# T4's weight parts split behind the first tile's B22, attention differences on VectorE, w_out's scaling at other ticks, and attention's closing additions behind a reciprocal

## The chip, the cores and the metric

One Trainium2 chip, one of its cores. The time is the device time of one execution in microseconds (us). A core has TensorE (PE, the matmuls; its weight loads are listed as PEld), VectorE (DVE), ScalarE (ACT), GpSimd (POOL), a queue engine SyncE (SP) and 16 DMA engines.

## The reference

One layer of a decoder trunk on x of 2048 rows and 1024 columns, all in fp32 (16 query heads, 2 key and value heads of width 64, window 128):

```python
shift, scale, gate = jnp.split(jax.nn.silu(c) @ w_ada + b_ada, 3, axis=-1)
u = x * (1.0 + scale) + shift
q, k, v, a_gate, p_in, p_gate, m_a, m_p = jnp.split(u @ w_in, offsets, axis=-1)
a = (sliding_window_sink_attention(q, k, v, sinks, bias, mask) * silu(a_gate)) @ w_attn_proj
p = einsum("bsgc,gcd->bsgd", multiscale_causal_pool(p_in), w_pool_mix)
p = ((p * pool_scale) * silu(p_gate)) @ w_pool_proj
y = ((sigmoid(m_a) * a + sigmoid(m_p) * p) @ w_out) * (1.0 + gate)
out = layer_norm(alpha * x + y, ln_gain, ln_bias)
```

## The kernel before

**Products.** Every large matrix product is computed in quads: two weight tiles of 128 columns against two halves of 512 rows of activations, with seven block products instead of eight: B11, T1, T2, B21, T3, B22, T4. Each is `product`: twelve fp32r matmuls of 128x512, because weights and activations are both split in a high and a low part (high by high, high by low, low by high). Twelve matmuls at full clock take 2.72 us. The weights come as a tile `W` (four blocks, three of which are made from differences by `sum1`, `mid` and `late` on POOL) and a tile `A22` (for T4). `pair_split` splits the weights of two products at once: ACT casts the high part into a `w_set` buffer (L303), and DVE makes the low part (L132, 128x1024). `half_split` does the same for one T4 (L310 and L132, 128x512). Products accumulate in banks of PSUM that the programs call `mm` and `lg` by their tags (four and two banks). Within a quad, T2 ends with the addition b = c + p5 (L365) and T3 with p5 = c + p5 (L387), both on DVE; T3 and T4 go on in the bank c.

**The order.** In `front` PE runs B11 and T1 of the two quads of a group, in `back` T2 and B21 of both, then T3 and B22 of the first, T3 and B22 of the second, and T4 of both. `ring` runs `front` of the next group behind `back`. The work of the other engines stands in program order on each engine; `tick` runs the side work (hooks) between products, `defer` moves a call some ticks on. A call of nc.vector, nc.scalar or nc.gpsimd may be moved by the tile scheduler; the wrapped ones (L57) keep their order.

**Stages, by the trace.** A head to 62 us, the first phase (gates of half 0) to 252, attention of half 0 to 600, the second phase to 830, attention of half 1 to 1178, then six phases: the last gates, the attention projection of half 0 (to 1290), the pool projection of half 0 (to 1370), the same two of half 1 (to 1448 and 1529), and the output product with LayerNorm. The four projection phases have two groups of two quads each. In them `take` on DVE multiplies the results by gates into tiles `wide`, the pool phases with two operations (L624 into `g`, L626 into `wide`), and DVE also makes the low parts of the next phase's activations (`set_B`, `set_T`).

**Attention.** 64 steps of two heads by 128 queries per half, with parts of steps n, n-1, n-2 and n-3 in flight at once. In a step, DVE runs: the reciprocal of the sums (`sm`), two additions into `o`, two maximum reductions over scores (`CUSTOM_DVE_ANT_0`), the low part `ptl` of the transposed probabilities, and the scaling of one head's probabilities (`L<-L,sm`). Beside the attention, `filling` runs products of other quads, a quarter product (three matmuls) at a time, five or six to a step; their weights are split by `split` (ACT, and POOL or DVE). Their two closing additions stand in `ended`, that is, in the program directly behind the last quarter of T2 or T3. `later(n, f)` runs f at the end of step n. `sums_between` is one such: at three places in each attention it fetches a row pair of the attention result into two `room` tiles and forms four differences of 128x512 (`sums_to`, on POOL: T1, T2, T4, T3), which are stored for the next phase.

**w_out.** In the second phase `sums_to` also prepares w_out in four parts (wo0 to wo3): two row blocks each are fetched into `spare`, multiplied by the gate row `cb` on DVE (`spare<-spare,cb`, 128x1024, twice per part), stored, and subtracted on POOL. The ticks at which the parts start are the last four numbers of a list.

## Time and profile before

| | |
|---|---|
| median of 3 runs | 1691.07 us (1689.7 to 1692.35) |
| the profiled execution, and its span | 1694.21 us, 1692.1 us |
| PE busy | 1645.3 us (97% of the span), 8058 matmuls |
| DVE busy | 1190.4 us (70%) |
| ACT busy | 1024.3 us (61%) |
| POOL busy | 968.4 us (57%) |
| mean granted PE clock | 0.997 of full speed |
| HBM | 197 GB/s over the span |

Busy time counts instructions that run, and with matmuls that are pipelined their ends are modelled. In the timeline a row gives the start, the time, the engine, the line, the operation, its output and inputs, and in square brackets the idle time ahead of it and the instruction that ended it. A row such as `lg<-set_T,w_set ... x12` is one block product. Line numbers from 205 on stand up to 14 higher in the kernel after the change (L132 and L57 stay, L615 becomes L620, L586 becomes L591).

### The profile page before, as it was taken

Reading aid. Unit: us, or ns where it says so; the run is one execution under the profiler, and the core shown is the slowest. Engines: PE = TensorE matmul, PEld = TensorE weight load, DVE = VectorE, ACT = ScalarE, POOL = GpSimd, SP = SyncE. Lnnn points to the kernel's source line nnn. Section 1 sums busy time; section 2 is a strip of 40 time slices with the busy share of each in tenths; the row PEclk is TensorE's granted clock in tenths of the full one; section 3 lists DMA queues with packets and bytes.
Section 4 is the critical chain, followed back from the end, with each engine's and each line's share of the span. In section 5 each row is a group of like instructions: output and inputs, shape, how many; then the busy total and the mean of one; then the engine's idle time right before and its main releaser. Section 6 shows DMA issues by size and latency. Waiting matters only on the chain.

```text
span 1692.1 us, 24664 instructions
## 1 busy us (share of the span) xinstructions
PE 1645.3 (97%) x8058; PEld 1383.4 (82%) x8058; DVE 1190.4 (70%) x2132; ACT 1024.3 (61%) x2146; POOL 968.4 (57%) x734
## 2 busy tenths in 40 slices
PE   7999999999999999999999999999999999999997
PEld 6788888888888788878888888887877878787886
DVE  6845656677767666486567677675768896978777
ACT  4754547877777655335578777776746454544452
POOL 3333437685867948764476768598444463323442
PEclk9999999999999999999999999999999999999999
DMA  9688844333442688872533345345957885676443
GB/s 360 218 281 301 206 152 139 97 123 115 159 148 69 223 280 295 290 260 101 167 112 107 111 127 179 106 148 186 357 201 272 290 307 193 238 276 232 150 150 112
DMA packets 185969, 331.55 MB, mean 196 GB/s; under 512 B 18016, under 2 KB 43760, under 8 KB 185840
## 3 DMA queue, kind: packets, MB, share of 16 engines
q1 hardware_dynamic: 182720, 325.72, 56.3%
q10 hardware_dynamic: 3088, 4.23, 1.2%
q8 instruction: 64, 1.05, 0.2%
q14 instruction: 65, 0.53, 0.1%
q0 software_dynamic: 32, 0.02, 0.0%
HBM read 223.77 MB, written 109.28 MB: 197 GB/s over the span
## 4 chain that ended last, share of the span: by engine, by line
PE 76%; DVE 9%; ACT 5%; DMA 4%; issue 3%; POOL 2%; SPq 1%; POOLq 0%; DVEq 0%; ACTq 0%
PE mm L57 49%; PE lg L57 20%; PE pv L57 4%; PE pt L57 3%; DVE set_T L57 1%; DMA ma_d<-raw 1%; DVE w_set L132 1%; ACT L L57 1%; DMA g<-ma_d 1%; DVE w_set L57 1%; ACT w_set L57 1%; DVE g L624 1%; SPq L57 1%; DVE L L57 1%; DVE qs L57 1%
## 5 line engine op out<-in xcount | busy, mean ns | idle before, releaser
L57 PE MATMUL mm<-set_B,w_set 128*128 128x512 f32 x2664 | 653.2, 392 | 0.6 <-DVE w_set L57 0.5
L57 PEld LDWEIGHTS mm<-set_B,w_set 128*128 128x128 f32 x2664 | 496.6, 188 | 103.0 <-DVE w_set L57 0.9
L57 PE MATMUL mm<-set_T,w_set 128*128 128x512 f32 x1824 | 453.9, 395 | 8.1 <-DVE mm L57 6.0
L57 PE MATMUL lg<-set_T,w_set 128*128 128x512 f32 x1704 | 413.8, 392 | 14.3 <-DVE w_set L132 12.4
L57 PEld LDWEIGHTS mm<-set_T,w_set 128*128 128x128 f32 x1824 | 335.9, 188 | 77.8 <-DVE mm L57 11.5
L57 PEld LDWEIGHTS lg<-set_T,w_set 128*128 128x128 f32 x1704 | 319.9, 189 | 86.5 <-DVE w_set L132 16.3
L132 DVE TENSOR_TENSOR w_set<-W,w_set 128x1024 fp32r<-128x1024 f32 x137 | 193.5, 1413 | 141.8 <-ACT w_set L303 131.8
L303 ACT CAST w_set<-W 128x1024 fp32r<-128x1024 f32 x137 | 143.8, 1050 | 195.1 <-PE mm L57 146.0
L266 POOL TENSOR_TENSOR W<-W,A 128x512 f32<-128x512 f32 x46 | 74.3, 1615 | 273.9 <-DMA A<-in_win_dram 65.2
L57 POOL TENSOR_TENSOR w_set<-W,w_set 128x512 fp32r<-128x512 f32 x120 | 157.5, 1320 | 100.3 <-ACT w_set L57 93.7
L57 DVE TENSOR_TENSOR o<-pv,o 64x128 f32<-64x128 f32 x256 | 72.0, 281 | 134.9 <-ACT o L57 128.4
L57 POOL TENSOR_TENSOR W<-W 128x512 f32<-128x512 f32 x82 | 108.3, 1335 | 46.3 <-DVE sm L57 25.6
L57 ACT ACTIVATE L<-L,nm 128x257 f32<-128x257 f32 (+1 forms) x256 | 127.2, 499 | 12.4 <-DVE nm L57 3.6
L275 POOL TENSOR_TENSOR W<-W 128x512 f32<-128x512 f32 x46 | 72.1, 1566 | 103.3 <-DVE w_set L132 91.5
L57 DVE CUSTOM_DVE_ANT_0 L<-lg,bt,nsink 128x256 f32<-128x256 f32 (+1 forms) x256 | 111.6, 473 | 20.2 <-PE lg L57 7.1
L270 POOL TENSOR_TENSOR W<-W 128x512 f32<-128x512 f32 x44 | 75.3, 1714 | 78.1 <-DVE w_set L132 69.0
L57 ACT CAST w_set<-W 128x512 fp32r<-128x512 f32 (+1 forms) x165 | 101.8, 628 | 27.7 <-POOL W L57 16.7
L57 ACT COPY o<-pv 64x256 f32<-64x256 f32 x128 | 47.3, 369 | 78.6 <-PE pv L57 77.5
L271 POOL TENSOR_TENSOR W<-W 128x512 f32<-128x512 f32 x44 | 69.2, 1572 | 33.2 <-DMA W<-in_win_dram 20.3
L57 DVE TENSOR_TENSOR ptl<-pt,pth 128x512 fp32r<-128x512 f32 (+1 forms) x128 | 85.6, 669 | 1.3 <-ACT pth L57 1.0
L57 POOL TENSOR_TENSOR spare<-spare 128x512 f32<-128x512 f32 x48 | 77.6, 1623 | 11.6 <-ACT spare L57 5.7
L57 ACT ACTIVATE L<-L,sm 128x256 f32<-128x256 f32 (+1 forms) x128 | 64.3, 502 | 31.5 <-DVE sm L57 31.2
(233 smaller groups left out, 2419.0 us busy)
## 6 DMA issues: line engine op xcount, KB each, us to landing
W<-in_win_dram SPq DMA_DIRECT2D x42, 512.0 KB, 5.9
W<-in_win_dram SPq DMA_DIRECT2D x42, 256.0 KB, 4.1
A<-in_win_dram SPq DMA_DIRECT2D x42, 256.0 KB, 4.8
ag_d<-sig SPq DMA_DIRECT2D x32, 256.0 KB, 5.3
pg_d<-sig SPq DMA_DIRECT2D x32, 256.0 KB, 5.0
pg<-pg_d SPq DMA_DIRECT2D x32, 256.0 KB, 3.3
pin_B<-fin SPq DMA_DIRECT2D x32, 256.0 KB, 2.1
ag<-ag_d SPq DMA_DIRECT2D x32, 256.0 KB, 2.9
```

Source lines behind the costliest of these rows:

```text
L57: return lambda *args, **kw: self.tc.keep_in_program_order(op(*args, **kw))
L132: engine.tensor_tensor(dst, src, as32(hi), ALU.subtract)
L266: e.tensor_tensor(self.w[:, 1, :], self.w[:, 2, :], self.a22, ALU.add)
L270: e.tensor_tensor(x[:, 1, :], x[:, 1, :], x[:, 0, :], ALU.subtract)
L271: e.tensor_tensor(x[:, 2, :], x[:, 0, :], x[:, 2, :], ALU.subtract)
L275: e.tensor_tensor(x[:, 3, :], x[:, 3, :], x[:, 1, :], ALU.subtract)
L303: a.copy(by_two(hi), raw)
L624: nc.vector.tensor_tensor(g, src, g, ALU.mult)
```

## The change

It has four parts.

1. `back`: where a group's quads have `ahead` (the two projections, both halves: phases 1 to 4 of the last six), both T4s' weights are split between the first quad's B22 and the second quad's T3, and the second quad's `third` pair ahead of the first's B22. Elsewhere the order stays. PE's order is the same everywhere.
2. In the attentions the four differences of `sums_between` run on DVE, their ticks are rounded up instead of down, and the second of the three places starts a step earlier.
3. The closing additions in attention are put in a list `closing` by `filling`; `close` issues them directly behind the reciprocal of the next step, or ahead of the next T3 or T4 if they are still in the list by then.
4. The four parts of w_out start at 33, 36, 43 and 48 instead of 34, 39, 44 and 50, and the second scaling of a part comes 1.5 ticks behind the first instead of 0.5. The same offset holds for the one other user of `work`, the modulation of x in the first phase.

```diff
--- before.py
+++ after.py
@@ -196,7 +196,7 @@
     def put(q, store, name, i, src):
         q.dma_start(store[name][i // 2, :, i % 2, :], src)
 
-    def sums_to(ph, store, i, load, work=None):
+    def sums_to(ph, store, i, load, work=None, eng=pool):
 
         b = []
 
@@ -210,11 +210,11 @@
                 load(b[r], r)
 
         def sub(out, a, c):
-            return lambda: pool.tensor_tensor(x(*out), x(*a), x(*c), ALU.subtract)
+            return lambda: eng.tensor_tensor(x(*out), x(*a), x(*c), ALU.subtract)
 
         todo = [(0, fetch)]
         if work:
-            todo += [(4, lambda: work(b[0], 0)), (4.5, lambda: work(b[1], 1))]
+            todo += [(4, lambda: work(b[0], 0)), (5.5, lambda: work(b[1], 1))]
         made = [("B11", (0, 0)), ("B21", (1, 0)), ("B22", (1, 1))] if work else []
         puts = [(5 + 0.6 * n, *x) for n, x in enumerate(made)]
         at = 7.5 if work else 4
@@ -393,15 +393,20 @@
             tick()
             q.consume(ph, 0, 1, b)
 
-        for x in range(len(st)):
-            third(x)
-            with_t3(x)
-            with_b22(x)
-        for q in nxt[len(st) :]:
-            ask(q)
+        lasts = []
+        third(0)
+        with_t3(0)
+        if grp[0].ahead:
+            third(1)
+            with_b22(0)
+            lasts = [half_split(ph, q.a22) for q in grp]
+        else:
+            with_b22(0)
+            third(1)
+        with_t3(1)
+        with_b22(1)
         for q, b, c, p5 in st:
-            w = half_split(ph, q.a22)
-            product(c, w, "T4")
+            product(c, lasts.pop(0) if lasts else half_split(ph, q.a22), "T4")
             tick()
             q.consume(ph, 1, 0, c)
 
@@ -929,25 +934,33 @@
             if name == "T1":
                 p5 = st[x][3] = tp.tile([P, CH], F32, tag="p5", bufs=2, name="p5")
                 act.copy(p5, b)
-            elif name == "T2":
-                dve.tensor_tensor(b, c, p5, ALU.add)
-            elif name == "T3":
-                dve.tensor_tensor(p5, c, p5, ALU.add)
             elif name == "B21":
                 take(x, 0, 0, a)
             elif name == "B22":
                 take(x, 0, 1, b)
-            else:
+            elif name == "T4":
                 take(x, 1, 0, c)
                 take(x, 1, 1, p5, True)
+
+        closing = []
+
+        def close():
+            while closing:
+                x, name = closing.pop()
+                _, b, c, p5 = st[x]
+                dve.tensor_tensor(b if name == "T2" else p5, c, p5, ALU.add)
 
         def filling():
             for i, (x, name) in enumerate(seq):
                 begun(i)
+                if name in ("T3", "T4"):
+                    close()
                 w = made.pop(i)
                 acc = st[x][{"B11": 0, "B21": 0, "T1": 1, "B22": 1}.get(name, 2)]
                 for k in range(4):
                     product(acc, w, name, name in ("B11", "T1"), k, k + 1)
+                    if k == 3 and x < K and name in ("T2", "T3"):
+                        closing.append((x, name))
                     yield
                 ended(i)
 
@@ -994,13 +1007,13 @@
             split(j)
 
         def sums_between(n0, i):
-            for offset, f in [(0, rooms), *sums_to(ph, ain_d[s], i, load_raw(ain_d[s], i))]:
-                later(n0 + int(offset / 2), f)
+            for offset, f in [(0, rooms), *sums_to(ph, ain_d[s], i, load_raw(ain_d[s], i), eng=dve)]:
+                later(n0 + math.ceil(offset / 2), f)
 
         def rooms():
             ph.turns["spare"] = iter([kvp.tile([P, D], F32, tag=f"qs0{t}", name=f"room{t}") for t in range(2)])
 
-        for i, n0 in enumerate((39, 56, 61)):
+        for i, n0 in enumerate((39, 55, 61)):
             sums_between(n0, i)
         fill = filling()
         lgs, exps, Ls, pvs, outs, ags = {}, {}, {}, {}, {}, {}
@@ -1018,6 +1031,7 @@
             if n - 1 in exps:
                 sm = exps[n - 1][2]
                 dve.reciprocal(sm, sm)
+            close()
             if n - 3 in pvs:
                 pv = pvs.pop(n - 3)
                 jj, tt, bb = (n - 3) // U, (n - 3) // NB % 2, (n - 3) % NB
@@ -1497,7 +1511,7 @@
                 lambda x, r: dve.tensor_tensor(x, x, cb, ALU.mult),
             ))
         ahead, hooks = hooks, {}
-        for start, todo in zip((14, 18, 22, 26, 30, 34, 39, 44, 50), side):
+        for start, todo in zip((14, 18, 22, 26, 30, 33, 36, 43, 48), side):
             for offset, f in todo:
                 at = int(start + offset) - 14
                 hooks.setdefault((at // 14, at % 14), []).append(f)
```

On DVE in the last group of the attention projection of half 0 (around 1280 us), the split of the two T4 weights (`w_set<-A22`) stood behind T3's additions of the first and the second quad (p5_13167 and p5_13215; W_13030 is the second quad's third pair):

```order
L387 TENSOR_TENSOR p5_13167<-lg_13168,p5_13167 128x512
L132 TENSOR_TENSOR w_set_13306<-W_13030,w_set_13305 128x1024
L615 TENSOR_TENSOR wide5_12572<-p5_13167,g_13161 128x512
L57 TENSOR_TENSOR set_T1_67<-set_T1_67 128x2x512
L615 TENSOR_TENSOR wide4_12571<-mm_13092,g_13206 128x512
L57 TENSOR_TENSOR set_T2_234<-set_T2_234 128x2x512
L387 TENSOR_TENSOR p5_13215<-lg_13216,p5_13215 128x512
L132 TENSOR_TENSOR w_set_13347<-A22_12990,w_set_13347 128x512
L615 TENSOR_TENSOR wide7_12574<-p5_13215,g_13165 128x512
L57 TENSOR_TENSOR set_T2_234<-set_T2_234 128x2x512
L615 TENSOR_TENSOR wide6_12573<-mm_13130,g_13210 128x512
L132 TENSOR_TENSOR w_set_13367<-A22_13031,w_set_13367 128x512
```

and now, with W_13015 in the place of W_13030 and A22_13016 of A22_13031:

```order
L132 TENSOR_TENSOR w_set_13289<-W_13015,w_set_13288 128x1024
L57 TENSOR_TENSOR set_B11_66<-set_B11_66 128x2x512
L387 TENSOR_TENSOR p5_13167<-lg_13168,p5_13167 128x512
L57 TENSOR_TENSOR set_T1_67<-set_T1_67 128x2x512
L620 TENSOR_TENSOR wide5_12572<-p5_13167,g_13161 128x512
L132 TENSOR_TENSOR w_set_13314<-A22_12990,w_set_13314 128x512
L620 TENSOR_TENSOR wide4_12571<-mm_13092,g_13206 128x512
L132 TENSOR_TENSOR w_set_13317<-A22_13016,w_set_13317 128x512
L57 TENSOR_TENSOR set_T2_234<-set_T2_234 128x2x512
L387 TENSOR_TENSOR p5_13215<-lg_13216,p5_13215 128x512
```

The third pair of the second quad stands ahead of the first T3's addition instead of behind it, and both low parts for T4 stand ahead of the second T3's addition; the gate products of the second quad (wide7, wide6) come behind.

On DVE at the 36th reciprocal of the first attention (439.83 us), the closing addition of a T2 (`mm_4471<-mm_4473,p5_4526`; sm_4515 are the sums of that reciprocal) stood at the end of the step, behind the scaling of L:

```order
L57 TENSOR_TENSOR ptl_4570<-pt_4556,pth_4569 128x512
L57 TENSOR_SCALAR L_4513<-L_4513,sm_4515 128x256
L57 TENSOR_TENSOR mm_4471<-mm_4473,p5_4526 128x512
L57 SCALAR_TENSOR_TENSOR fin_4468<-fin_4468,mm_4129 128x512
L57 RECIPROCAL sm_4574<-sm_4574 128x2
```

and now it stands behind the step's reciprocal, ahead of the additions into o:

```order
L57 TENSOR_SCALAR L_4439<-L_4439,sm_4441 128x256
L57 SCALAR_TENSOR_TENSOR fin_4384<-fin_4384,vb_4376 128x512
L57 RECIPROCAL sm_4515<-sm_4515 128x2
L57 TENSOR_TENSOR mm_4471<-mm_4473,p5_4526 128x512
L57 TENSOR_TENSOR o_4504<-pv_4543,o2_4565 64x128 x2
L57 ISA L_4573,nm_4574<-lg_4551,bt_3952,nsink_71 128x256
```

It has moved ahead by one step's work on DVE, which follows it in the same order.

On DVE in the second phase around 746 to 760 us, in the group of k, v and the first q, the two scalings of wo3 (`spare<-spare,cb`) stood behind the low part of W_7567 (the second quad's first pair, `front`):

```order
L132 TENSOR_TENSOR w_set_7646<-W_7519,w_set_7645 128x1024
L586 TENSOR_SCALAR sig_7593<-sig_7593,psc_72 128x512
L586 TENSOR_SCALAR sig_7621<-sig_7621,psc_72 128x512
L132 TENSOR_TENSOR w_set_7683<-W_7567,w_set_7682 128x1024
L586 TENSOR_SCALAR sig_7642<-sig_7642,psc_72 128x512
L57 TENSOR_TENSOR spare_7614<-spare_7614,cb_6526 128x1024
L57 TENSOR_TENSOR spare_7613<-spare_7613,cb_6526 128x1024
L132 TENSOR_TENSOR w_set_7726<-W_7519,w_set_7725 128x1024
L132 TENSOR_TENSOR w_set_7776<-W_7567,w_set_7775 128x1024
```

and now, with W_7523 and W_7579 in the place of W_7519 and W_7567:

```order
L132 TENSOR_TENSOR w_set_7648<-W_7523,w_set_7647 128x1024
L591 TENSOR_SCALAR sig_7603<-sig_7603,psc_72 128x512
L57 TENSOR_TENSOR spare_7572<-spare_7572,cb_6526 128x1024
L57 TENSOR_TENSOR spare_7571<-spare_7571,cb_6526 128x1024
L591 TENSOR_SCALAR sig_7625<-sig_7625,psc_72 128x512
L132 TENSOR_TENSOR w_set_7689<-W_7579,w_set_7688 128x1024
L591 TENSOR_SCALAR sig_7644<-sig_7644,psc_72 128x512
L132 TENSOR_TENSOR w_set_7729<-W_7523,w_set_7728 128x1024
L132 TENSOR_TENSOR w_set_7778<-W_7579,w_set_7777 128x1024
```

They stand two gate rows and one low part earlier, ahead of the second quad's first pair instead of behind it, and still next to each other.

## Prediction

> **What bounds the kernel.** I read the page's busy shares first, then PE's waits, then the windows around the places where the waits lie, then the timeline at each.
>
> ```profile
> PE 1645.3 (97%) x8058; PEld 1383.4 (82%) x8058; DVE 1190.4 (70%) x2132; ACT 1024.3 (61%) x2146; POOL 968.4 (57%) x734
> ```
>
> PE is the bound, and no matmul is added or removed. So the change can only give or take PE's idle time and slow clock. PE's waits (what PE waited for: us in total, times, longest):
>
> ```profile
> PE lg L57 <- DVE w_set L132: 12.4, 9, 2.8
> PE pv L57 <- DMA head_qs<-in_wadat_dram: 7.9, 1, 7.9
> PE mm L57 <- DVE mm L57: 6.0, 5, 2.1
> PE pt L57 <- DMA head_B<-in_wadat_dram: 3.1, 1, 3.1
> PE mm L57 <- DVE sm L57: 2.1, 1, 2.1
> PE pv L57 <- DVE ptl L57: 1.5, 4, 0.6
> ```
>
> The two DMA waits are the head, which isn't touched. The first line (a low part that DVE makes) is what parts 1 and 4 aim at; the third and fifth (T3 waits for T2's closing addition) are part 3's. Here the first line's large members stand: PE at the T4s of the attention projection of half 0 (1280), the pool projection (1363), the same of half 1 (1442, 1521).
>
> ```profile
> 1277.66 2.88 PE L57 MATMUL mm<-set_B,w_set 128*128 128x512 f32 x12
> 1280.38 1.98 PE L57 MATMUL lg<-set_T,w_set 128*128 128x512 f32 x8
> 1284.47 5.51 PE L57 MATMUL lg<-set_T,w_set 128*128 128x512 f32 x16 [2.11 <-DVE w_set L132]
> ...
> 1363.81 3.06 PE L57 MATMUL lg<-set_T,w_set 128*128 128x512 f32 x12 [1.30 <-DVE w_set L132]
> 1368.55 1.20 PE L57 MATMUL lg<-set_T,w_set 128*128 128x512 f32 x4 [1.68 <-DVE w_set L132]
> ...
> 1442.54 3.03 PE L57 MATMUL lg<-set_T,w_set 128*128 128x512 f32 x12 [0.26 <-DVE w_set L132]
> 1446.57 1.21 PE L57 MATMUL lg<-set_T,w_set 128*128 128x512 f32 x4 [1.00 <-DVE w_set L132]
> ...
> 1521.35 3.06 PE L57 MATMUL lg<-set_T,w_set 128*128 128x512 f32 x12 [1.01 <-DVE w_set L132]
> 1527.18 2.08 PE L57 MATMUL lg<-set_T,w_set 128*128 128x512 f32 x4 [2.77 <-DVE w_set L132]
> 1529.05 3.56 PE L57 MATMUL mm<-set_B,w_set 128*128 128x512 f32 x12
> ```
>
> Each T4 stops after its eight high matmuls, because the low part isn't there. Twelve matmuls last 2.88 us, yet the next product starts 2.72 behind (1280.38 less 1277.66), so a row's end lies 0.16 past the point where PE could go on: each stall costs its bracket and 0.16 more. Two stalls have a tail. After 1284.47, sixteen matmuls take 5.51 where the pitch of 0.227 (2.72 over 12) gives 3.79, and after 1527.18 the 2.08 and 3.56 stand against 1.07 (2.88 less eight times 0.227) and 2.88: 1.7 us more each. The windows (us, then busy time and instructions of PE, PEld, DVE, ACT and POOL, the granted clock, DMA share, GB/s) show why:
>
> ```profile
> 1275.00:1301.00 26.00, 23.89 (x99) 19.31 (x98) 23.35 (x20) 11.49 (x14) 13.06 (x8) 0.93 0.94 335
> 1345.00:1381.00 36.00, 33.02 (x145) 26.65 (x144) 35.13 (x36) 20.50 (x28) 15.91 (x9) 1.00 0.94 339
> 1433.00:1460.00 27.00, 25.75 (x112) 20.62 (x112) 25.02 (x23) 15.97 (x22) 11.81 (x7) 1.00 0.79 284
> 1512.00:1543.00 31.00, 27.22 (x112) 21.77 (x111) 28.84 (x28) 14.18 (x18) 11.45 (x8) 0.94 0.93 333
> 1284.40:1288.00 3.60, 3.53 (x9) 2.78 (x10) 3.60 (x6) 2.59 (x3) 0.00 (x0) 0.54 1.05 398
> 1527.10:1531.00 3.90, 3.82 (x10) 3.09 (x11) 3.47 (x5) 0.00 (x0) 1.27 (x1) 0.57 0.98 339
> ```
>
> In the two short windows the granted clock was 0.54 and 0.57. In the four long ones DVE is full or nearly so: 2.65, 0.87, 1.98 and 2.16 us are free. So at these places DVE's queue, not PE, sets the pace, and an earlier low part pushes something else back.
>
> **Part 1, T4's low parts earlier.** The four places lose 2.11 + 0.16 + 1.7 = 3.97, then 1.30 + 1.68 + 0.32 = 3.30, then 0.26 + 1.00 + 0.32 = 1.58, and 1.01 + 2.77 + 0.32 + 1.7 = 5.80: 14.65 in all, the ceiling of this part. Nothing is added; both low parts now stand ahead of the second T3's closing addition, which T4 of the second quad needs, and of the gate products and the next front's low part, which stood between or behind them. In the attention projections (1280 and 1442) DVE has 2 to 2.65 us free and the gate products there take one operation per result, so I take nearly all: 3.7 and 1.5. In the pool projections a result takes two operations, the same work stays in the stretch, and the wait partly changes its name: the second T4 waits for the second T3's addition, then the front for its low part. With 0.87 free at 1345 I take half, 1.7; at 1512, with 2.16 free and the clock's 1.7 regained if no single stall is as long as 2.1, I take 3.5. Together 10.4 (4 if DVE's queue gives back only its free time and no clock, 14.65 if all goes). ACT's casts for the T4s move up too, ahead of two casts for `set_T2`; at 44% to 59% busy ACT has the room.
>
> **Part 3, closing additions.** The first attention's example, DVE and then PE:
>
> ```profile
> 439.83 0.16 DVE L57 RECIPROCAL sm<-sm 128x2 f32<-128x2 f32 x1
> 440.83 0.58 DVE L57 TENSOR_TENSOR o<-pv,o 64x128 f32<-64x128 f32 x2 [0.84 <-ACT o L57]
> ...
> 442.87 1.39 DVE L57 TENSOR_SCALAR L<-L,sm 128x256 f32<-128x256 f32 x1
> 444.18 0.69 DVE L57 TENSOR_TENSOR mm<-mm,p 128x512 f32<-128x512 f32 x1
> ```
> ```profile
> 444.92 1.45 PE L57 MATMUL mm<-set_T,w_set 128*128 128x512 f32 x5 [1.63 <-DVE mm L57]
> ```
>
> The addition runs last in the step, and T3 waits for it. Behind the reciprocal it falls in the 0.84 us in which DVE waits for ACT, and T3 finds it done. By the order, four of the six T3 stalls are of this kind, the four of the third waits line less its longest: 6.0 - 2.1 = 3.9, and 4 x 0.16 = 0.6: 4.5 gained. The other two (one in each attention, 2.1 each, that longest and the fifth waits line) keep their place in the order. In the first attention it looks like this on POOL, ACT and PE:
>
> ```profile
> 566.96 1.28 POOL L57 TENSOR_TENSOR room<-room 128x512 f32<-128x512 f32 x1
> 568.32 1.28 POOL L57 TENSOR_TENSOR room<-room,room 128x512 f32<-128x512 f32 x1
> ```
> ```profile
> 574.81 0.62 ACT L57 CAST w_set<-W 128x512 fp32r<-128x512 f32 x1 [2.16 <-POOL W L57]
> ```
> ```profile
> 579.31 0.97 PE L57 MATMUL mm<-set_T,w_set 128*128 128x512 f32 x3 [2.08 <-DVE sm L57]
> ```
>
> ACT stood 2.16 us at a weight that POOL made late, after two differences of 1.28 that part 2 takes away, and everything behind it on ACT and DVE came late. That frees up to 2.56 there, so between 0 and 2 x (2.08 + 0.16) = 4.5 comes back; I take half, 2.2. The cost of part 3 is an addition that stood in time and comes later:
>
> ```profile
> 338.76 0.17 DVE L57 RECIPROCAL sm<-sm 128x2 f32<-128x2 f32 x1
> ```
> ```profile
> 338.92 1.30 PE L57 MATMUL mm<-set_T,w_set 128*128 128x512 f32 x5
> ```
>
> This T3 started at 338.92; its addition now starts behind the reciprocal, at about 338.9 (338.76 + 0.17), and lasts 0.69: it ends near 339.6. That is 0.7 lost in each attention, 1.4 (0 if the step's earlier work moves up by the 0.69 that left it, 3 with neighbours alike). Net of part 3 and that effect of part 2: 4.5 + 2.2 - 1.4 = 5.3.
>
> **Part 2, 24 differences on DVE.** Each is an operation like the addition, 0.69, or like the scaling above that lasts 1.39 where POOL works beside it: 16.6 to 33 us of DVE, four per place, one or two to a step. The cover is DVE's wait ahead of the o additions:
>
> ```profile
> L57 DVE TENSOR_TENSOR o<-pv,o 64x128 f32<-64x128 f32 x256 | 72.0, 281 | 134.9 <-ACT o L57 128.4 <-POOL w_set L57 2.7 <-issue 1.1
> ```
>
> 134.9 us in 128 steps, 1.05 a step. One difference of 0.69 fits in a mean step; I take 0, and if the cover were gone it would be the whole 17.
>
> The Trainium skill, "SBUF — State Buffer", section "SBUF: two separate sides", says that a DVE operation with two SBUF inputs and a GpSimd operation that reads SBUF exclude each other for a whole instruction. The scaling's 1.39 would fit waiting of that kind; by it a difference on DVE would cost 1.28 less on POOL and up to that again on DVE, inside the bound of 33 given above.
>
> **Part 4, w_out.** DVE and PE in the group of k and v:
>
> ```profile
> 749.00 2.30 DVE L132 TENSOR_TENSOR w_set<-W,w_set 128x1024 fp32r<-128x1024 f32 x1
> ...
> 752.66 4.55 DVE L57 TENSOR_TENSOR spare<-spare,cb 128x1024 f32<-128x1024 f32 x2
> ```
> ```profile
> 751.01 2.88 PE L57 MATMUL mm<-set_B,w_set 128*128 128x512 f32 x12
> ...
> 759.50 1.21 PE L57 MATMUL lg<-set_T,w_set 128*128 128x512 f32 x4 [1.08 <-DVE w_set L132]
> ```
>
> Two scalings of 2.3 held the low part that T2 needed: 1.08 + 0.16 lost. That goes: +1.2. Now they stand ahead of the low part of 749.00, still together. It was done at 751.30, and its product B11 needs it behind eight matmuls, at 751.01 + 8 x 0.227 = 752.8. With 4.55 ahead of it, it would be done at 755.85 at worst, 3.0 late; the earlier start of wo3 may take all of that away, since DVE has gaps in the group. So it is between 1.2 - 3.0 = -1.8 and +1.2; I take +1.0, near the upper end, because wo3 starts two of a group's 14 ticks earlier (48 against 50), and a tick is a product of 2.72. In the first phase the same offset moves an ACT operation by a tick; no PE wait of the list lies there, 0.
>
> **Sum.** 10.4 + 5.3 + 0 + 1.0 = 16.7. From the profiled execution (1694.21, span 1692.1) that makes 1677.5; it stands 3.1 above the median of 1691.07, and from the median it makes 1674.4.
>
> **Rivals.**
> *The waits change their names (faster, less).* DVE was full at the four places; if only its free time (2.65, 0.87, 1.98, 2.16) could be used, and the second quad's addition and the next front's low part are late by nearly what the T4s gain, part 1 gives 4 instead of 10.4. Against it: two of four places have one gate operation per result, and the late work there isn't PE's next. 1691.07 - 10.3 = 1680.8.
> *Attention's chain grows (slower).* In each step DVE's line reciprocal, o, maxima, ptl, scaling feeds PE, and 52 additions and 24 differences now stand in it ahead of what PE waits for. If 0.69 of each that doesn't fit reaches PE, the gain of 16.7 is gone at 25 of the 76 (16.7 / 0.69); with 30 the time is 1691.07 - 16.7 + 20.7 = 1695.1. Against it: the mean step has 1.05 idle at just that point, and PE's list shows only 1.5 us for waits on `ptl`.
> *w_out isn't spread.* By the order the scalings stay adjacent and now precede the front's own low part; if PE meets them with 3.0 of stall, 1.8 net of the 1.2, and the rest goes as forecast, the time is 1691.07 - 15.7 + 1.8 = 1677.2.
> *The slow clock stays.* Clock 0.54 stood behind 2.11 us of idle PE, while the T3 stall of 2.08 at 579.31 has three matmuls in 0.97, not slow. If the slow stretches come by their own rhythm and not from these stalls, 3.4 stays: 1677.8. The Trainium skill, "TensorE: Matmul & The Clock Gate", Part 1, states such a rule: the clock halves after an idle window of about 3.4 us that runs freely. The two stalls here are shorter than that, and the trace has them slow all the same, so the trace speaks for the stalls.
>
> **Chances and range.** Forecast (1669 to 1677) 0.42, waits renamed 0.22, w_out 0.12, clock 0.07, attention slower 0.13, no change because gains and new stalls cancel 0.04. What a measurement of this kernel can tell from no change is about 0.2%, 3.4 us. Faster: 0.42 + 0.22 + 0.12 + 0.07 = 0.83; same 0.04; slower 0.13. Low end: part 1 at 14.65 (+4.25), the two 2.1 stalls wholly gone (+2.3), no new ones (+1.4) give 1666.5. High end: waits renamed (1680.8) with w_out's -1.8 (+2.8) and the new attention stalls doubled (+1.4) is 1685.0, and some unlisted wait more: 1687. The range 1666.5 to 1687 leaves the slower cases out.
>
> **What would show it.** Right: the line of lg for DVE's L132 falls from 12.4 to about 5, the lines for DVE's mm and sm from 8.1 to 3 or 4, and no stretch with a clock near 0.55 at the T4s. Renamed: a line of lg for p5's addition (L387 before) or of mm for L132 grows at the fronts behind the T4s. w_out: a stall near 753. Attention wrong: waits of pv on ptl, or of pt on DVE's scaling of L, rise from 1.5, and the first attention lasts longer than its 348 us (252 to 600).

## The result and the profile after

The changed kernel took 1680.33 us (median of 6, 1679.79 to 1682.62), the kernel before in the same runs 1691.28: a ratio of 0.9935 (95% interval 0.9922 to 0.9948), or 11.0 us faster (8.8 to 13.2). The forecast was 16.7 faster, 1674.4. The profiled execution took 1681.68 us with a span of 1679.9.

PE's waits in the changed kernel, without the two DMA waits of the head and those under 0.8 us:

```profile
PE lg L57 <- ACT w_set L303: 2.8, 2, 1.5
PE pv L57 <- ACT pth L57: 2.4, 4, 1.4
PE lg L57 <- DVE p L387: 2.3, 1, 2.3
PE pv L57 <- DVE ptl L57: 2.0, 5, 0.6
PE mm L57 <- DVE mm L57: 1.2, 3, 0.5
PE lg L57 <- DVE w_set L132: 0.9, 2, 0.7
PE mm L57 <- DVE sm L57: 0.9, 2, 0.4
```

The two lines that the change aims at, 12.4 and 8.1 before, are 0.9 and 2.1 (the second is two lines here): 17.5 us of waits are gone. Four lines are new or longer: a weight cast of ACT (2.8), the addition of p5 (2.3), ACT's cast of the probabilities (2.4 against 0.8), and `ptl` (2.0 against 1.5). PE in the pool projections, around the T4s (of half 0, then half 1):

```profile
1354.58 1.20 PE L57 MATMUL lg<-set_T,w_set 128*128 128x512 f32 x4 [0.68 <-DVE w_set L132]
1357.02 3.00 PE L57 MATMUL lg<-set_T,w_set 128*128 128x512 f32 x12 [1.23 <-ACT w_set L303]
...
1362.19 1.19 PE L57 MATMUL mm<-set_B,w_set 128*128 128x512 f32 x4 [0.36 <-DVE w_set L132]
...
1507.39 1.97 PE L57 MATMUL lg<-set_T,w_set 128*128 128x512 f32 x8
1509.62 1.19 PE L57 MATMUL lg<-set_T,w_set 128*128 128x512 f32 x4 [0.25 <-DVE w_set L132]
1513.14 4.53 PE L57 MATMUL lg<-set_T,w_set 128*128 128x512 f32 x12 [2.33 <-DVE p L387]
```

The second T4 now waits as a whole, ahead of its first matmul, 1.23 and 2.33 us (the first is named after a cast of ACT that ends at 1356.91; DVE's addition of p5, which this T4 needs, ends at 1356.87). Behind the second stall twelve matmuls take 4.53 us instead of 2.88. In the attention projection of half 1 both T4s run without a stop:

```profile
1431.23 5.60 PE L57 MATMUL lg<-set_T,w_set 128*128 128x512 f32 x24
```

The windows that answer to the four of before, then the slow stretch (us; busy time and instructions of PE, PEld, DVE, ACT, POOL; clock, DMA share, GB/s):

```profile
1268.00:1294.00 26.00, 25.92 (x115) 21.17 (x114) 24.39 (x22) 14.54 (x20) 15.20 (x8) 1.00 0.97 360
1336.00:1372.00 36.00, 33.73 (x147) 26.98 (x146) 35.55 (x35) 21.87 (x29) 14.29 (x9) 1.00 0.91 314
1424.00:1451.00 27.00, 27.00 (x121) 22.36 (x120) 24.60 (x22) 18.21 (x25) 17.38 (x8) 1.00 0.80 282
1500.00:1531.00 31.00, 28.42 (x118) 22.77 (x117) 30.44 (x29) 16.28 (x20) 12.22 (x8) 0.94 0.96 337
1513.10:1517.30 4.20, 4.16 (x12) 3.34 (x13) 4.20 (x7) 1.04 (x1) 0.00 (x0) 0.60 0.47 176
```

PE fills the first and the third (attention projections). In the second and the fourth (pool projections) DVE is the full one, 0.45 and 0.56 us free, and PE loses 2.3 and 2.6.

Both kernels run the same 8058 matmuls in the same order, so each matmul's start can be set against its start before ("by the starts" below). Where this difference moves, set against the first trace of before:

| stage | forecast, us | these two traces, us |
|---|---|---|
| head | 0 | +0.6 |
| attention of half 0 | -2.6 | -1.6 |
| second phase (w_out), with the wait for keys at its end | -1.0 | -2.2 |
| attention of half 1 | -2.7 | -2.0 |
| first group of the attention projection, half 0 | 0 | +0.3 |
| T4s: attention projection, half 0 | -3.7 | -3.6 |
| T4s: pool projection, half 0 | -1.7 | -0.5 |
| T4s: attention projection, half 1 | -1.5 | -1.9 |
| T4s: pool projection, half 1 | -3.5 | -1.2 |
| sum (of the rows before rounding) | -16.7 | -12.2 |

### The profile page after: what moved, and what is told of

Read it like the earlier page. It is cut to its first block, busy times and chain, and to the rows that moved or that the text cites. A ratio compares the mean times of both kernels' runs of the same rounds, so it can differ in the third digit from the quotient of the medians.

```text
span 1679.9 us, 24661 instructions
## 1 busy us (share of the span) xinstructions
PE 1642.9 (98%) x8058; PEld 1382.7 (82%) x8058; DVE 1208.6 (72%) x2156; ACT 1026.3 (61%) x2146; POOL 949.3 (57%) x710
## 4 chain that ended last, share of the span: by engine, by line
PE 80%; DVE 7%; DMA 5%; ACT 3%; issue 2%; POOL 2%; SPq 1%; POOLq 0%; DVEq 0%; ACTq 0%
PE mm L57 51%; PE lg L57 22%; PE pv L57 4%; PE pt L57 4%; DMA head_T<-in_wada_dram 1%; DMA g<-mp_d 1%; DVE w_set L132 1%; DVE L L57 1%; SPq L57 1%; DVE set_T L57 1%; DMA head_B<-in_wada_dram 1%; DVE room L57 1%; DVE w_set L57 0%; DMA g<-ma_d 0%; ACT g L609 0%
## 5 line engine op out<-in xcount | busy, mean ns | idle before, releaser
L57 DVE TENSOR_TENSOR o<-pv,o 64x128 f32<-64x128 f32 x256 | 71.9, 281 | 96.8 <-ACT o L57 93.4
L57 POOL TENSOR_TENSOR W<-W 128x512 f32<-128x512 f32 x82 | 111.1, 1368 | 52.8 <-DVE sm L57 25.8
L275 POOL TENSOR_TENSOR W<-W 128x512 f32<-128x512 f32 x46 | 71.9, 1563 | 103.9 <-DVE w_set L132 94.0
L270 POOL TENSOR_TENSOR W<-W 128x512 f32<-128x512 f32 x44 | 80.3, 1828 | 83.1 <-DVE w_set L132 66.7
L271 POOL TENSOR_TENSOR W<-W 128x512 f32<-128x512 f32 x44 | 69.1, 1570 | 32.4 <-DMA W<-in_win_dram 16.4
```

Of the source, the lines that this page charges most:

```text
L57: return lambda *args, **kw: self.tc.keep_in_program_order(op(*args, **kw))
L270: e.tensor_tensor(x[:, 1, :], x[:, 1, :], x[:, 0, :], ALU.subtract)
L271: e.tensor_tensor(x[:, 2, :], x[:, 0, :], x[:, 2, :], ALU.subtract)
L275: e.tensor_tensor(x[:, 3, :], x[:, 3, :], x[:, 1, :], ALU.subtract)
```

## The experiments

Ratios are to the kernel before in runs on the same chip, with 95% intervals; a difference in us is the ratio's.

**The four parts, each alone on the kernel before.** The hunks are those of the diff.

*Part 1 alone:*

```diff
-        for x in range(len(st)):
-            third(x)
-            with_t3(x)
-            with_b22(x)
...
+            third(1)
+            with_b22(0)
+            lasts = [half_split(ph, q.a22) for q in grp]
```

> The kernel before with part 1 alone. If the parts add up, as a comparison of the two traces matmul by matmul has it (the projection phases gained 3.8, 0.6, 1.6 and 1.3 us and lost 0.4 ahead of them), this gains 6.9: 1684.4 against 1691.3. If the wait at the last T4 (2.33 us for p5's addition, and a slow clock behind it) comes from the other parts' shift in time, it isn't there, and the gain is nearer the forecast's 10.4: 1680.9.

1684.75 us, ratio 0.9962 (0.9948 to 0.9976): 6.4 faster. The wait for p5's addition is there without the other parts:

```profile
PE lg L57 <- DVE p L387: 2.1, 1, 2.1
```

So the new wait belongs to part 1 and doesn't come from the other parts' shift in time.

*Part 3 alone:*

```diff
+            close()
             if n - 3 in pvs:
```

> The kernel before with part 3 alone. By the forecast the four T3 stalls go (4.5) and two new ones of 0.7 come (1.4): 3.1 gained, 1688.2, and the two stalls of 2.1 near 579 and 1156 us stay. If GpSimd sets the pace of 530 to 566 us (it is busy without a gap there in both traces), what is gained before 530 is lost again at about 566: then about 1.5 to 2 gained, 1689.5.

1691.07 us, ratio 0.9994 (0.9984 to 1.0003): 1.0 faster, not told from nothing. The four stalls are gone, the stalls near 579 and 1153 us stay (2.07 each), and the feared one is there:

```profile
340.33 0.97 PE L57 MATMUL mm<-set_T,w_set 128*128 128x512 f32 x3 [0.50 <-DVE mm L57]
...
579.03 0.96 PE L57 MATMUL mm<-set_T,w_set 128*128 128x512 f32 x3 [2.07 <-DVE sm L57]
```

The interval reaches from 2.7 faster to 0.5 slower; the 3.1 of the forecast lies outside, the 1.5 to 2 of the rival inside. In this trace the stall of 2.07 near 1153 has a slow stretch of the clock behind it, which neither trace of the kernel before has there.

*Part 2 alone:*

```diff
-            return lambda: pool.tensor_tensor(x(*out), x(*a), x(*c), ALU.subtract)
+            return lambda: eng.tensor_tensor(x(*out), x(*a), x(*c), ALU.subtract)
...
-        for i, n0 in enumerate((39, 56, 61)):
+        for i, n0 in enumerate((39, 55, 61)):
```

> The kernel before with part 2 alone. If the two T3 stalls of 2.1 near 579 and 1156 us come from GpSimd's differences, they shrink to about 0.4 each as in the changed kernel: 3 to 3.5 gained, 1688. If they shrank through part 3, they stay, and the time is that of before, 1691.3, or up to 1 more from 24 more operations on VectorE.

1688.47 us, ratio 0.9981 (0.9970 to 0.9992): 3.2 faster. The T3 near 579 us starts without a wait, the one near 1156 with 0.43 instead of 2.07:

```profile
579.80 0.84 PE L57 MATMUL mm<-set_T,w_set 128*128 128x512 f32 x3
```

So the two stalls came from GpSimd's differences (the edit also moves their ticks, and the two effects weren't run apart), and part 2 is a gain by itself. But GpSimd pays for it. Its operations that now meet a difference on DVE take longer, here the first trace of before and this one:

```profile
558.10 1.06 POOL L57 TENSOR_TENSOR nxt<-vb 128x526 f32<-128x526 f32 x1
558.27 1.51 POOL L57 TENSOR_TENSOR nxt<-vb 128x526 f32<-128x526 f32 x1
```

By the starts PE loses 0.98 near 566 us and 0.85 near 1144 to waits for ACT's cast of the probabilities, which comes late behind GpSimd.

*Part 4 alone:*

```diff
-            todo += [(4, lambda: work(b[0], 0)), (4.5, lambda: work(b[1], 1))]
+            todo += [(4, lambda: work(b[0], 0)), (5.5, lambda: work(b[1], 1))]
...
-        for start, todo in zip((14, 18, 22, 26, 30, 34, 39, 44, 50), side):
+        for start, todo in zip((14, 18, 22, 26, 30, 33, 36, 43, 48), side):
```

> The kernel before with part 4 alone. Forecast 1.0 gained; the traces showed 1.7 (stalls of 0.15 and 1.08 with the 0.16 behind each, and 0.2 more): 1689.6. By the rival (w_out not spread, with a stall at the second quad's first pair near 753 us) 1 to 2 lost: 1692.5 to 1693.

1690.78 us, ratio 0.9997 (0.9988 to 1.0007): 0.5 faster, not told from nothing. The stall of 1.08 is gone and none comes near 753 us. But this trace has slow stretches behind the stalls of 2.08 and 2.07 near 579 and 1156 us, which this part doesn't touch: 1.4 and 1.35 by the starts. In the changed kernel DVE shows why w_out's stall is gone:

```profile
742.78 2.45 DVE L57 TENSOR_TENSOR spare<-spare,cb 128x1024 f32<-128x1024 f32 x2 [0.92 <-DMA spare<-in_wout_dram]
...
746.59 2.31 DVE L132 TENSOR_TENSOR w_set<-W,w_set 128x1024 fp32r<-128x1024 f32 x1
```

The two scalings take 2.45 together, not 4.55, and the low part behind them is done at 748.90; its B11 starts at 749.55. The sum of the four alone is 6.4 + 1.0 + 3.2 + 0.5 = 11.1, and the whole change gave 11.0. Each of the four is known to about 2 us only, so that they meet this closely is partly luck.

**The kernel before, once more.** Nothing is edited.

> The kernel before, once more, for a second trace of it. In the traces of the three kernels that leave the projections as they were, PE waits 7.4 to 7.7 us at the four T4 places, not 10.1 as in the first trace, and the slow stretch behind the stall at 1284 us is missing. If the first trace was a dear execution (it stood 3.1 us over the median), this one waits 7 to 8 us there and its slow stretches lie elsewhere. If it is the usual one, it waits 10 us again and the clock falls again behind the stalls at 1284 and 1527 us.

It took 1690.56 us, against 1694.21 of the first trace, and the stalls differ:

```profile
PE lg L57 <- DVE w_set L132: 9.4, 8, 2.8
```
```profile
1282.71 4.15 PE L57 MATMUL lg<-set_T,w_set 128*128 128x512 f32 x16 [0.87 <-DVE w_set L132]
```

9.4 instead of 12.4 us. At 1282 PE waits 0.87 where the first trace had 2.11, and the sixteen matmuls behind it aren't slow (4.15 against 5.51). At the T4 places it waits 0.87, 1.32 + 1.72, 0.31 and 1.37 + 2.81, 8.4 us against 10.1. So 3.7 us of the first trace were that execution's own, and by the starts 3.2 of them lie at the very places that part 1 was priced at (2.6 and 1.1 in the two attention projections, 0.5 the other way in the last pool projection).

**The second low part behind p5's addition**, an edit of the changed kernel:

```diff
-            lasts = [half_split(ph, q.a22) for q in grp]
+            lasts = [half_split(ph, grp[0].a22)]
...
         with_t3(1)
+        if lasts:
+            lasts.append(half_split(ph, grp[1].a22))
```

> The changed kernel, with the second quad's T4 weights split behind that quad's T3 instead of ahead of it, so that p5's addition comes ahead of the second low part. If only the order of the two was wrong, the waits for p5's addition in the pool phases (2.3 us at 1513, 1.2 at 1357) fall to about 0.5 and nothing takes their place: 3 us faster than the changed kernel, 1677. If VectorE's queue is the bound there (no gap from 1501 to 1519 us), the next front's low part comes as late as now, PE waits about 2 us for it instead, and the time is within 1 us of the changed kernel's 1680.3.

1681.37 us, ratio 0.9936 (0.9919 to 0.9952), the changed kernel's own. PE at the last T4s and the front behind them:

```profile
1508.67 2.88 PE L57 MATMUL lg<-set_T,w_set 128*128 128x512 f32 x12
1513.15 2.98 PE L57 MATMUL lg<-set_T,w_set 128*128 128x512 f32 x12 [1.60 <-DVE p L387]
...
1519.53 1.21 PE L57 MATMUL mm<-set_B,w_set 128*128 128x512 f32 x4 [1.58 <-DVE w_set L132]
```

The first T4 doesn't stop any more, p5's addition still comes 1.60 late, and the front waits 1.58 for its low part, which it hadn't done there. The wait changes its name with the order, and DVE's queue is the bound.

**T4's low parts on GpSimd**, an edit of the changed kernel:

```diff
-            lasts = [half_split(ph, q.a22) for q in grp]
+            lasts = [half_split(ph, q.a22, nc.gpsimd) for q in grp]
```

> The changed kernel, with the two T4 low parts of the projection phases made on GpSimd instead of VectorE. This takes 3.5 us (two of 1.77) out of VectorE's full stretch ahead of the last T4, and 2 to 3 in the other pool phase. If VectorE's queue is the bound, the waits for p5's addition go and the fronts aren't late: 3 to 5 us faster than the changed kernel, 1676. If GpSimd's additions slow VectorE by as much, or GpSimd's own queue is late with the next front's sums, the time is the same or up to 3 us longer.

1678.54 us, ratio 0.9920 (0.9905 to 0.9934): about 2.5 better than the changed kernel by the ratios, whose intervals overlap, and short of the 3 to 5. By the starts of the two traces the projections are 4.4 shorter, and 0.9 is lost at 830 us to a wait for keys that no edit touches (1.0 instead of 0.2). DVE in the same stretch:

```profile
1505.13 2.88 DVE L631 TENSOR_TENSOR wide<-g,wide 128x512 f32<-128x512 f32 x2
1507.93 2.30 DVE L57 TENSOR_TENSOR set_T<-set_T 128x1024 fp32r<-128x1024 f32 x1
1510.16 0.68 DVE L387 TENSOR_TENSOR p<-lg,p 128x512 f32<-128x512 f32 x1
```

Two operations of DVE fewer, but those left beside GpSimd's are longer: the two `wide` take 2.88 (1.28 in the changed kernel), `set_T` 2.30 (1.21). The wait for p5's addition is still 1.57 there.

**GpSimd's sums a tick later**, an edit of the changed kernel:

```diff
-            if x < len(nxt):
+            if x < len(nxt) and not (x and grp[0].ahead):
                 ask(nxt[x])
...
             lasts = [half_split(ph, q.a22) for q in grp]
+            if len(nxt) > 1:
+                ask(nxt[1])
```

> The changed kernel, with the second quad's loads for the next group (and with them GpSimd's two sums) asked for a tick later in the projection phases, as before the change. In the changed kernel these sums run beside VectorE's two low parts for T4 near 1508 us, and each low part took 1.74 us. If the sums beside them make them long, and this makes the wait for p5's addition, the low parts take 0.7 to 0.9, the addition comes 1.7 to 2 us earlier, the wait of 2.33 shrinks to about 0.5 and the clock stays up there: 3 us faster than the changed kernel, 1677.3. If VectorE's queue is the bound and the length of these two is not what counts, or the front's sums come late instead, the time is 1679.5 to 1681.

1681.22 us, ratio 0.9945 (0.9930 to 0.9960), not faster. The sums didn't move: the first starts at 1507.67, released by DVE's `wide`, against 1507.63. So this says nothing on sums that run elsewhere. It still shows one thing, DVE in that stretch:

```profile
1507.26 2.38 DVE L132 TENSOR_TENSOR w_set<-A,w_set 128x512 fp32r<-128x512 f32 x2
1509.56 2.30 DVE L57 TENSOR_TENSOR set_T<-set_T 128x1024 fp32r<-128x1024 f32 x1
```

The low parts take 2.38 together, against 3.47 in the changed kernel, with a start that is 0.5 earlier while the sums stand where they were; `set_T` now meets the sums and takes 2.30 for 1.21. The delay goes to whatever stands there, and p5's addition is 2.50 late.

**Attention: two more low parts on VectorE**, an edit of the changed kernel that also puts the addition near 340 us ahead of its reciprocal again:

```diff
-                on_dve |= {(x, "T3"), (x, "T4"), (x + 1, "T2"), (x + 1, "T3")}
+                on_dve |= {(x, "T3"), (x, "T4"), (x + 1, "T2"), (x + 1, "T3"), (x + 1, "B22"), (x + 1, "T4")}
...
+                        if now_n[0] == 15 and name == "T2":
+                            close()
```

> The changed kernel with two edits in attention: two more low parts per large pooling window go from GpSimd to VectorE, and the closing addition near 340 and 912 us stands ahead of the reciprocal again. If GpSimd's gapless stretch is what gives the gain back near 567 us, the waits there (1.4 and 0.6 us) fall to 0.7 or less together, and the stalls near 340 and 912 (0.5 and 0.44) go: 2 to 2.5 us faster than the changed kernel, 1678. If VectorE's chain is the limit there, the four more low parts of 0.7 make the wait longer, and the time is 1680 to 1682.

1692.3 us, ratio 1.0004 (0.9995 to 1.0013): all of the gain lost, far past both expectations. PE, then DVE:

```profile
554.75 1.65 PE L57 MATMUL mm<-set_T,w_set 128*128 128x512 f32 x3 [6.04 <-DVE mm L57]
```
```profile
552.33 1.75 DVE L57 TENSOR_TENSOR w_set<-A,w_set 128x512 fp32r<-128x512 f32 x1 [1.15 <-ACT w_set L57]
554.01 0.69 DVE L57 TENSOR_TENSOR mm<-mm,p 128x512 f32<-128x512 f32 x1
```

T2's closing addition ends up behind two moved low parts. The one shown waits 1.15 us for ACT's cast and takes 1.75; another, at 545.27, waits 1.13 and takes 1.51. That is 5.5 us, and the addition comes 5.6 later than the changed kernel's (548.39). T3 waits 6.04 us (5.33 in the other attention), with a slow clock behind it. The waits near 567 and 340 us did go, and the cure was worse: what was moved waits for another engine, and DVE's queue waits with it.

**Attention: two multiplications instead**, an edit of the changed kernel with the same edit near 340 us:

```diff
-                pool.tensor_tensor(o, o, ags.pop(x), ALU.mult)
+                (dve if n in (50, 54) else pool).tensor_tensor(o, o, ags.pop(x), ALU.mult)
```

> The changed kernel with two edits in each attention: the closing addition near 340 and 912 us stands ahead of the reciprocal again, and two gate multiplications of 128x512 (o by ag) go from GpSimd to VectorE ahead of GpSimd's gapless stretch. Neither waits for a cast of ScalarE, as the low parts that were moved in the run before did. If GpSimd's queue is the cause of the waits near 567 us (1.4 and 0.6), two operations of 1.3 less bring them under 0.8 together, and with 0.5 and 0.44 at the two T3s the gain is 2 to 2.5: 1678. If it isn't, only the 0.9 of the T3s comes: 1679.4.

1677.83 us, ratio 0.9917 (0.9901 to 0.9934): about 3.0 better than the changed kernel by the ratios, whose intervals overlap. The waits near 567 and the T3 stalls near 340 and 912 are gone, so GpSimd's queue was the cause near 567. But waits of 0.89 and 0.36 come at 544 instead, and similar ones near 1118: the waits for ACT's cast of the probabilities are 2.4 us in all, as in the changed kernel. By the starts the gain lies at the T3s (0.8 near 340, 0.7 each near 912, 578 and 1151), not in the moved multiplications.

**Both together:**

> The edits of the last expectation and T4's low parts on GpSimd in the projections together. The two touch different stages, so the gains should add: 1680.3 less 1.8 and less 2.2, 1676.3. If they don't add (a later stage waits for a transfer instead, as the second attention's start did with 1 us for its first keys), 1677.5 to 1678.5.

1676.09 us, ratio 0.9907 (0.9889 to 0.9926), 15.7 faster than before. **With the sums a tick later as well:**

> The kernel with T4's low parts on GpSimd and the two attention edits (1676.1), with the same loads and sums a tick later. If sums beside VectorE's operations are what is left of the waits for p5's addition (1.43 and 0.66 us), it gains 1 to 1.5: 1674.8. If the low parts on GpSimd now lie where the sums lay, nothing changes, 1676.1, and with the next front's sums late it is 1 slower.

1675.29 us, ratio 0.9910 (0.9892 to 0.9928): the same. These two are the fastest kernels of this study, both under the changed kernel's 1680.33.

## Why the prediction was right, and where it was wrong

The direction and the range held, and each part took away most of the stalls that it aimed at. The sum was 16.7 and the measured gain 11.0, so the time lies outside the forecast's own band (1669 to 1677, 0.42) and at the rival "the waits change their names" (1680.8, 0.22). By the prediction's own signs both came: the lines of waits fell further than for "right", and the line for p5's addition grew from 0.2 to 2.3 as for "renamed", with a slow stretch at the last T4. The rival's mechanism is there in part 1; that its number fits to 0.5 us is luck, for it had 4, 5.3 and 1.0 for part 1, parts 2 and 3, and part 4, where 6.4, 4.2 and 0.5 were measured.

**Part 1 failed in size: 10.4 forecast, 6.4 measured alone (4.1 to 8.8).** Two steps of its term were wrong.

The first is "The four places lose ... 14.65 in all, the ceiling of this part". That is what they lost in one execution. The prediction notes that this execution stood 3.1 us over the median, and then takes terms measured in it off the median. The second trace of before has 8.4 us of T4 waits instead of 10.1 and one slow stretch instead of two. By the same rule (0.16 for each of six stalls, 1.7 for one slow stretch) its ceiling is 8.4 + 1.0 + 1.7 = 11.1.

The second is "at 1512, with 2.16 free and the clock's 1.7 regained if no single stall is as long as 2.1, I take 3.5". The free time of a window is an average; DVE's queue there has no gap ahead of the addition that counts. DVE in the changed kernel:

```profile
1507.79 3.47 DVE L132 TENSOR_TENSOR w_set<-A,w_set 128x512 fp32r<-128x512 f32 x2
1511.18 1.21 DVE L57 TENSOR_TENSOR set_T<-set_T 128x1024 fp32r<-128x1024 f32 x1
1512.31 0.68 DVE L387 TENSOR_TENSOR p<-lg,p 128x512 f32<-128x512 f32 x1
```

The two low parts cost 3.47 us, 1.74 each, beside GpSimd's sums, where the stretch before had 1.16 and 0.67. They stand ahead of the addition, and the second T4 waited 2.33 with a slow clock behind it. Of 3.5 came 1.2, of the 1.7 in the other pool projection 0.5. In the two attention projections 3.6 and 1.9 came (3.7 and 1.5 forecast), but 2.6 and 1.1 of these are what the first trace had and the second hadn't: against the second trace the four places, in the order of the table, gained 1.1, 0.5, 0.8 and 1.7. The rival "the waits change their names" is what happened in the pool phases, and the run with the second low part behind the addition bears it out: another order, the wait shared between the addition and the front's low part, the same time.

**Part 3: 3.1 forecast, 1.0 measured alone (-0.5 to 2.7).** In the trace of that part alone the four stalls went (5.0 by the starts, 4.5 forecast). The new stall came at its place with 0.50, by the starts 0.8 and 0.7 in the two attentions, for the 0.7 forecast. Three things were left out. PE also loses 0.4 near 440, 0.5 near 550 and 0.3 at 566 us. A slow stretch behind the stall near 1153, which this part leaves in place, costs 1.55 in this trace. And slow stretches were more frequent in this part's executions: their mean granted clock is 0.9954, against 0.9963 for the kernel before in the same runs, which over 1690 us makes an estimated 1.5 us. Why they were is open.

The loss at 566 is a gain given back. GpSimd sets the pace from 530 to 566 us, in the changed kernel 35.06 of 36 us busy:

```profile
530.00:566.00 36.00, 35.21 (x189) 29.76 (x187) 26.83 (x67) 24.03 (x70) 35.06 (x29) 1.00 0.44 137
```
```profile
566.85 0.51 PE L57 MATMUL pv<-pth,vv 128*128 128x256 f32 x2 [1.40 <-ACT pth L57]
```

PE came there 0.8 us earlier than before, GpSimd 0.7 later (two of its operations ahead of that place took 2.72 instead of 2.19), and PE waited 1.40 for a cast of ACT that stands behind a weight which GpSimd makes. The 0.8 is part 3's and the 0.7 is part 2's: by the starts PE loses 0.3 there with part 3 alone, 1.0 with part 2 alone, where it comes no earlier than before, and 1.3 with both. The prediction didn't look at who sets the pace between the stalls that it removed. With two multiplications less on GpSimd the wait at 566 is gone, which shows the cause, though most of it came back at 544.

**Part 2: 2.2 forecast, 3.2 measured alone (1.4 to 5.1).** Its trace gives 2.35 and 1.64 at the two stalls, 4.0 in all, where the forecast took half of 4.5; and it loses 1.8 at the waits near 566 and 1144, where the forecast took 0 for the 24 differences (a slow stretch of 1.5 behind the first of these waits not counted). The net meets the 2.2, but by two errors that cancel: luck. The cover held on DVE only, and the cost came on GpSimd. In the changed kernel the 24 differences take 14.6 + 10.4 = 25.0 us on DVE (1.04 each, inside the bounds of 0.69 and 1.39), and DVE's idle time ahead of the o additions is 96.8 instead of 134.9:

```profile
L57 DVE TENSOR_TENSOR o<-pv,o 64x128 f32<-64x128 f32 x256 | 71.9, 281 | 96.8 <-ACT o L57 93.4 <-issue 0.9
...
L57 DVE TENSOR_TENSOR room<-room 128x512 f32<-128x512 f32 x12 | 14.6, 1219 | 0.0
...
L57 DVE TENSOR_TENSOR room<-room,room 128x512 f32<-128x512 f32 x12 | 10.4, 865 | 0.1
```

The rival "attention's chain grows" (1695.1) didn't come: waits on `ptl` rose from 1.5 to 2.0 only, though those on `pth` rose from 0.8 to 2.4.

**Part 4: 1.0 forecast, 0.5 measured alone (-1.2 to 2.0).** The worst case of 3.0 rested on scalings of 2.3 each; they took 1.23 each at their new place, after 0.92 of waiting for their own rows, and the low part was still done 0.65 ahead of its B11. The stall that went was 1.08 in the first trace and 0.61 in the second, so this term was too large for the same reason as part 1's. The mean granted clock of this part's executions is 0.9952, against 0.9963: an estimated 1.8 us of slow clock that hides its gain.

**The clock.** The prediction held that a slow stretch follows a single stall of more than 2.1 us. Each of the two did stand behind its stall, but length alone doesn't decide (below): a stall of 2.07 has a slow stretch behind it in some traces, one of 2.43 in another has none. In the second trace the stall near 1283 was only 0.87 and its slow stretch wasn't there, and in the changed kernel the stall of 2.33 at 1513 brought one, 0.60 in the window above. So 3.4 of the sum couldn't be counted on, and the rival "by their own rhythm" was nearer than its 0.07: the rhythm is there, and a stall has to meet it.

## What to carry to other kernels

Price a stall from more than one execution, or scale the terms down to the median: an execution that stands 0.2% over it can have its surplus at the very stalls that one is about to price, as 3.2 of 3.7 us here. Where an engine's queue is gapless around a place, moving one of its operations ahead only gives the wait another name; what helps is to take work off that queue, and only work that doesn't itself wait for another engine. A stall taken away early in a stage is kept only if no other engine sets the pace later in it. And work moved to an engine with room can still lengthen what runs beside it on the engine that it left. A stall isn't priced by its length alone: one that put 1.85 us or more of idle time into one window of the clock cost 1.35 to 1.7 more.

## What the runs showed of the hardware

**The slow clock goes by windows of 3.41 us.** Between the head and 1660 us, a slow stretch is half of the full clock for 3.41 us, the length of eight matmuls of 128x512 at 0.427 us each (6.83 us, two in a row, behind the stalls of 6.04 and 5.33). Within one trace slow stretches begin whole numbers of 3.413 us apart: 71 in the first trace of before (1284.69 and 1527.04), 106 with part 1 alone (1155.95, 1517.77), 194 with part 2 alone (569.81, 1232.00), 107 with part 3 alone (1154.40, 1519.62), 169 and 107 with part 4 alone (579.95, 1156.80, 1522.03). So each execution has a grid of windows, and PE's busy time in them shows what a stall has to meet. First the trace of before, then part 2 alone:

```profile
1281.28:1284.69 3.41, 1.30 (x6) 0.79 (x5) 3.41 (x4) 0.28 (x1) 1.74 (x2) 1.00 1.03 390
1284.69:1288.10 3.41, 3.41 (x9) 2.66 (x9) 3.41 (x5) 2.41 (x3) 0.00 (x0) 0.50 1.06 397
```
```profile
566.40:569.81 3.41, 1.82 (x11) 1.39 (x12) 3.36 (x9) 3.27 (x10) 3.41 (x4) 1.00 0.03 10
569.81:573.22 3.41, 3.41 (x11) 2.73 (x10) 3.36 (x10) 3.01 (x9) 3.33 (x3) 0.50 0.71 268
1358.29:1361.70 3.41, 2.42 (x11) 1.68 (x9) 3.41 (x3) 0.83 (x1) 1.83 (x2) 1.00 0.52 165
1361.70:1365.12 3.42, 1.98 (x9) 1.64 (x10) 3.42 (x7) 0.55 (x1) 0.00 (x0) 1.00 0.89 291
1365.12:1368.53 3.41, 1.69 (x8) 1.09 (x7) 3.41 (x6) 2.40 (x3) 0.00 (x0) 1.00 0.87 249
```

The stall of 2.11 lies in one window, PE is busy for 1.30 of it, and the next window is slow. The stall of 2.43 is split by the border at 1361.70, no window has less than 1.69 us of busy PE, and the clock stays up:

```profile
1363.14 3.02 PE L57 MATMUL lg<-set_T,w_set 128*128 128x512 f32 x12 [2.43 <-DVE w_set L132]
1367.88 1.21 PE L57 MATMUL lg<-set_T,w_set 128*128 128x512 f32 x4 [1.72 <-DVE w_set L132]
```

In that part of all fourteen traces, each of the 18 windows in which PE was idle for 1.85 us or more was followed by a slow one, and of the 6538 with 1.83 or less only one was: the window at 566.40 above, with 1.59 of idle time in two waits. Why it counts is open. This also explains how one stall is dear in one execution and not in another: of the ten T3 stalls of 2.07 to 2.08 in the traces that have them, four have a slow stretch behind them. These four lie each in one window; the other six are split by a border. The Trainium skill, "TensorE: Matmul & The Clock Gate", Part 1, has a window of about 3.4 us that runs freely; the traces agree with that and with its length. The idle window that the page asks for isn't in them: windows with 0.6 to 1.8 us of busy PE were enough.

**An operation's length depends on its neighbour on another engine.** A 128x512 low part took 0.68 us with GpSimd idle and 1.74 beside its sums, and in the edits that moved it or its start, the operations that met GpSimd instead grew (`set_T` from 1.21 to 2.30, two `wide` from 1.28 to 2.88).
